# A two-layer hybrid encoder trunk: four places for the split weights, a fixed order of the first pieces, and conditioning sums on VectorE

## Chip, cores and metric

The kernel runs on one core of a Trainium2 chip. The metric is the device time of one execution in microseconds, lower is better. The profiled execution is one of several; every duration quoted below is of that one.

## What is computed

The reference is a trunk of two layers on 256 tokens of width 1024. Cut to what matters here:

```python
c_act = jax.nn.silu(c)                                   # c: 1 x 1024
for l in range(2):
    mod = c_act @ ada_w[l] + ada_b[l]                    # 1024 x 6144: the conditioning
    shift_m, scale_m, gate_m, shift_f, scale_f, gate_f = split(mod, 6)
    h = rms_norm(x, mix_norm_g[l]) * (1 + scale_m) + shift_m
    z = h @ w_in[l]                                      # 1024 x 7680: q, k, v of three mixers, and gates
    # differential, neighbourhood and dilated attention on parts of z
    merged = sum(sigmoid(gate_i) * (out_i @ w_proj_i))
    x = x + gate_m * (merged @ w_out[l])
    h = rms_norm(x, ffn_norm_g[l]) * (1 + scale_f) + shift_f
    x = x + gate_f * hier_moe(h)                         # 32 SwiGLU experts, top 2 within the best of 4 groups
return rms_norm(x, final_norm_g)
```

All weights are float32 in HBM, some 540 MB in all, and each is read once.

## The kernel before, in words

Each layer is a mixer stage and an expert stage. **The mixer** multiplies h by w_in in 15 chunks of 512 columns (function `chunk`); chunks 0 to 8 make q, k and v, chunks 9 to 14 the gates. A chunk's 2 MB of weights come as 1024x512 and are used in four pieces of 128x1024 elements. To keep float32 accuracy at TensorE's faster format, `split` (L322) makes two tiles of every piece: ScalarE casts it to `whi` (L327), VectorE subtracts to `wlo` (L330), and TensorE makes three products per block (`gemm`, L333): hi with whi, hi with wlo, lo with whi. A piece is 24 matmuls of 256 columns. `whi` and `wlo` have two buffers each (tags w4a, w4b), so a third piece can be split only when TensorE is done with the first. The two parts of h, `hi` and `lo`, are made by `modulated` (L277) for the eight 128-row blocks k: VectorE scales (L292), ScalarE adds the shift and rounds to hi (L294), VectorE makes lo (L289). Two pieces of chunk 0 are split ahead with GpSimd in place of VectorE for wlo (`early`).

`place` evacuates q and k with rotary embedding: four ScalarE copies per tile (L484), two VectorE multiplies (L485, L486) and a GpSimd addition (L487).

**The conditioning** is cut into 6 sections per layer, each of four parts of 1 MB (`ada_part`, L155). Sections 0 and 1 of layer 0 run at the start, on TensorE (L95, tile adap, with the silu of c as stationary operand of 32 columns). All others are mixed into the chunks by the table FILL: `ada_part` scales a part by c with ScalarE (L173) and VectorE (L175, 14 instructions of 128x512 per section), summing the parts of the section elementwise, and then sums over the 128 partitions with eight TensorE matmuls (adap<-rg,one), copies (L190), transposes (L193) and adds the bias (L195); the two gate sections go out to a row in HBM and come back as a broadcast tile `grb` (`gate_row`).

**The experts** (`moe`) read 8 groups of 12 tiles of 2 MB per layer (w13, w2g, w2c) and have little to compute on each.

Two things set the order. All DMAs of weights are issued by one queue (SP) in program order, each when a buffer is free: `slots` is a pool of 10 buffers of 16 KB per partition ("pairs"), which weights, conditioning parts and the long-lived tiles (xT, G, Q, K, V, T: six pairs in the mixer before) share; tiles of that pool all bear the name rg. And a list scheduler puts each engine's instructions in an order when the program is built; `keep_in_program_order` pins some of them. On the chip each engine runs its list in that order.

Of the kernel before, what the change touches and what calls it, by code (L numbers as in the profile page):

```python
# [21 lines left out]
P = 128  # L22
# [38 lines left out]
class Kernel:  # L61
# [91 lines left out]
    SEC = {0: ("col", 0), 1: ("col", 1), 2: ("row", 0), 3: ("col", 2), 4: ("col", 3), 5: ("row", 1)}  # L153

    def ada_part(self, l, s, h):  # L155

        nc = self.nc
        w = self.slot("ada").rearrange("p (j n) -> p j n", j=2)
        nc.sync.dma_start(w, self.io["ada_w"][l, s, h].rearrange("p (j n) -> p j n", j=2))
        kind, i = self.SEC[s]  # L160
        if h == 0:
            self.ada_ps = self.adap()
        ps = self.ada_ps[:, :256]
        if (l, s) in ((0, 0), (0, 1)):
            parts = [(w[:, j], self.scb[:, 2 * h + j, :], 2 * h + j) for j in range(2)]
        else:
            V = nc.vector
            for c in range(0, D, 512):
                cs = slice(c, c + 512)
                for j in range(2):  # L170
                    k, to = 2 * h + j, w[:, j, cs]
                    if j == 0 and h % self.CHAIN == 0:
                        nc.scalar.mul(to, to, self.sc[:, k:k + 1])  # L173
                    else:
                        V.scalar_tensor_tensor(to, to, self.sc[:, k:k + 1], w[:, 0, cs] if j else self.ada_sum[:, cs],  # L175
                                               op0=OP.mult, op1=OP.add)
            self.ada_sum = w[:, 1]
            parts = [(w[:, 1], self.one32, 2 * h + 1)] if (h + 1) % self.CHAIN == 0 else []
        for r, v, k in parts:
            ri = r.rearrange("p (m i) -> p i m", i=KD)  # L180
            for q in range(4):
                self.mm(ps[32 * q:32 * q + 32], v, ri[:, 2 * q:2 * q + 2, :] if s in (3, 4) else
                        r[:, 256 * q:256 * (q + 1)], k == 0 or k == 2 * self.CHAIN - 1 and v is self.one32, k == KD - 1)
        if h < 3:
            return
        if kind == "row":
            self.ada_row(l, i, ps, w[:, 0, :256])
            return
        sb = w[:, 0, :256]
# [188 lines left out]
    def mixer(self, l, fill):  # L378
# [63 lines left out]
        def chunk(n):  # L442
# [3 lines left out]
            if n == 4:  # L446
                late_loads()
# [681 lines left out]
```

## Time and profile before

| | before |
|---|---|
| time, median of 3 runs | 1534.49 us (1534.33 to 1534.7) |
| the profiled execution | 1535.39 us, of which the span shown is 1533.6 |
| TensorE (PE) busy | 1228.9 us, 80% |
| VectorE (DVE) busy | 606.8 us, 40% |
| ScalarE (ACT) busy | 384.7 us, 25% |
| GpSimd (POOL) busy | 73.4 us, 5% |
| HBM traffic | 543.93 MB, mean 355 GB/s |

The shares are means over stages that are unlike each other: two mixer stages (to about 345 us, and from 778 to 1095 us) and two expert stages. So the profile is read by stage. [...]

### The profile page before, as it was taken

Reading aid. Unit: us, or ns where it says so; the run is one execution under the profiler, and the core shown is the slowest. Engines: PE = TensorE matmul, PEld = TensorE weight load, DVE = VectorE, ACT = ScalarE, POOL = GpSimd, SP = SyncE. Lnnn points to the kernel's source line nnn. Section 1 sums busy time; section 2 is a strip of 40 time slices with the busy share of each in tenths; the row PEclk is TensorE's granted clock in tenths of the full one; section 3 lists DMA queues with packets and bytes.
Section 4 is the critical chain, followed back from the end, with each engine's and each line's share of the span. In section 5 each row is a group of like instructions: output and inputs, shape, how many; then the busy total and the mean of one; then the engine's idle time right before and its main releaser. Section 6 shows DMA issues by size and latency. Waiting matters only on the chain. (4 is left out here: it accounts for less than half of the span.)

```text
span 1533.6 us, 20114 instructions
## 1 busy us (share of the span) xinstructions
PE 1228.9 (80%) x8370; PEld 796.2 (52%) x8370; DVE 606.8 (40%) x1202; ACT 384.7 (25%) x681; POOL 73.4 (5%) x71
## 2 busy tenths in 40 slices
PE   5998999989777577677778899999897577577575
PEld 3888889874233133133257889899543133133132
DVE  2779884772112012011058797448322012011012
ACT  2656555450000000000046566544200000000001
POOL 1202000100000000000011110001000000000001
PEclk8999999999979889787889999999998788798898
DMA  9778683869999999999994874276899999999997
GB/s 369 284 296 319 275 326 146 343 246 403 428 425 427 427 427 427 427 426 428 421 372 172 340 312 186 110 315 235 318 425 426 427 426 427 427 426 427 426 427 294
DMA packets 52975, 543.93 MB, mean 355 GB/s; under 512 B 6784, under 2 KB 8336, under 8 KB 12048
## 3 DMA queue, kind: packets, MB, share of 16 engines
q1 hardware_dynamic: 52880, 542.60, 85.8%
q8 instruction: 68, 1.11, 0.3%
q14 instruction: 27, 0.22, 0.0%
HBM read 541.51 MB, written 1.06 MB: 354 GB/s over the span
## 5 line engine op out<-in xcount | busy, mean ns | idle before, releaser
L95 PE MATMUL acc<-rg,xg 128*32 128x512 f32 x2048 | 279.0, 687 | 116.3 <-DMA rg<-w 114.3
L95 PE MATMUL acc<-hi,wlo 128*128 128x256 f32 x896 | 260.0, 295 | 18.4 <-DVE wlo L330 18.0
L95 PE MATMUL acc<-lo,whi 128*128 128x256 f32 x896 | 253.4, 289 | 0.2 <-DVE lo L289 0.2
L95 PE MATMUL acc<-hi,whi 128*128 128x256 f32 x896 | 245.6, 290 | 6.5 <-ACT hi L294 4.9
L95 PE MATMUL acc<-rg,b 128*32 128x512 f32 (+1 forms) x1152 | 159.7, 688 | 93.7 <-DMA rg<-w2g 76.6
L95 PEld LDWEIGHTS acc<-rg,xg 128*32 128x32 f32 x2048 | 68.2, 118 | 303.7 <-issue 294.7
L330 DVE TENSOR_TENSOR wlo<-rg,whi 128x1024 fp32r<-128x1024 f32 x148 | 183.9, 1243 | 86.7 <-ACT whi L327 86.4
L327 ACT CAST whi<-rg 128x1024 fp32r<-128x1024 f32 x152 | 159.1, 1047 | 162.3 <-PE acc L95 136.1
L95 PEld LDWEIGHTS acc<-hi,wlo 128*128 128x128 f32 x896 | 175.1, 196 | 31.6 <-DVE wlo L330 24.2
L95 PEld LDWEIGHTS acc<-lo,whi 128*128 128x128 f32 x896 | 174.4, 196 | 1.6 <-DVE lo L289 0.5
L95 PEld LDWEIGHTS acc<-hi,whi 128*128 128x128 f32 x896 | 169.5, 196 | 10.5 <-ACT hi L294 5.5
L833 DVE TENSOR_TENSOR b<-b,acc 128x512 f32<-128x512 f32 x16 | 11.0, 687 | 350.5 <-PE acc L95 350.5
L95 PEld LDWEIGHTS acc<-rg,b 128*32 128x32 f32 x1152 | 35.5, 124 | 200.1 <-DMA rg<-w2g 112.6
L95 PEld LDWEIGHTS misc<-b,xn 128*128 128x128 f32 x512 | 124.6, 334 | 17.1 <-issue 15.7
L95 PE MATMUL misc<-b,xn 128*128 128x128 f32 x512 | 125.6, 404 | 4.1 <-DVEq L938 2.2
L832 ACT ACTIVATE b<-acc 128x512 f32<-128x512 f32 x16 | 9.6, 597 | 441.5 <-PE acc L95 441.5
L175 DVE SCALAR_TENSOR_TENSOR rg<-rg,sc 128x512 f32<-128x512 f32 x140 | 112.0, 832 | 4.4 <-DMA rg<-ada_w 2.5
L846 DVE TENSOR_TENSOR Y<-acc,grb 128x512 f32<-128x512 f32 x28 | 19.4, 692 | 235.5 <-PE acc L95 235.5
L826 ACT COPY b<-misc 128x256 f32<-128x256 f32 x16 | 6.0, 373 | 334.9 <-PE misc L825 334.9
L813 DVE TENSOR_SCALAR xg<-misc,mcol 128x128 f32<-128x128 f32 x128 | 44.3, 406 | 106.5 <-PE misc L95 106.5
L95 PE MATMUL acc<-wlo,hi 128*128 128x256 f32 (+1 forms) x256 | 79.8, 317 | 4.4 <-DVE wlo L330 4.3
L95 PE MATMUL acc<-whi,lo 128*128 128x256 f32 (+1 forms) x256 | 78.6, 314 | 1.5 <-DVE lo L310 1.3
(169 smaller groups left out, 1165.7 us busy)
## 6 DMA issues: line engine op xcount, KB each, us to landing
rg<-w SPq DMA_DIRECT2D x128, 2048.0 KB, 39.2
rg<-w2g SPq DMA_DIRECT2D x56, 2048.0 KB, 38.3
rg<-w_in SPq DMA_DIRECT2D x56, 1024.0 KB, 7.0
rg<-ada_w SPq DMA_DIRECT2D x48, 1024.0 KB, 8.5
rg<-w2c SPq DMA_DIRECT2D x12, 1024.0 KB, 29.6
rg<-w_proj SPq DMA_DIRECT2D x8, 1024.0 KB, 4.8
rg<-w_out SPq DMA_DIRECT2D x8, 1024.0 KB, 6.9
rg<-w_in SPq DMA_DIRECT2D x8, 512.0 KB, 15.4
```

The costliest lines, as they stand in the source:

```text
L95: return self.nc.tensor.matmul(out, lhsT, rhs, start=start, stop=stop, **kw)
L175: V.scalar_tensor_tensor(to, to, self.sc[:, k:k + 1], w[:, 0, cs] if j else self.ada_sum[:, cs], op0=OP.mult, op1=OP.add)
L327: c = nc.scalar.copy(whi, w)
L330: (nc.gpsimd if early else nc.vector).tensor_sub(wlo, w, whi.bitcast(F32))
L813: nc.vector.tensor_scalar(xg[:, k, :], p[:, kk * P:(kk + 1) * P], gf[:, k:k + 1], sf[:, k:k + 1], op0=OP.mult, op1=OP.add)
L826: nc.scalar.copy(ST, p[:, :256])
L832: nc.scalar.activation(a, h1, AF.Silu)
L833: nc.vector.tensor_mul(a, a, h3)
L846: nc.vector.tensor_mul(Y[:, hs], y[half], self.grb[:, hs])
```

## The change

- **Four places.** `split` takes its place from a list `homes`: during chunks 0 to 8 that is two halves of a pair ("parts") and the two old buffers in turn; later the old two alone. G shrinks to one long-lived tile (G2); the other two gate tiles are taken from the pool after the attention, in program order ("gates").
- **Order of the first pieces.** All four pieces of chunk 0 are split inside `modulated`, one before every second k, pinned in program order; wlo is always made by VectorE, none by GpSimd. One copy of xT goes from VectorE to ScalarE.
- **Conditioning.** ada_w lies transposed in HBM, so that one output is one row: c is broadcast to all partitions (`conditioning`, 512 KB, at the start and again in layer 1, as grb is overwritten by the gate rows in between), and VectorE multiplies and sums along the free axis with one `tensor_tensor_reduce` of 128x1024 for each half part (L166 of the new kernel; order lists show it as two rows, the operation and the read of its accumulator). No TensorE work, no transposes, no ScalarE scaling remains. Sections 0 and 1 of layer 0 are summed like the rest.

```diff
     def ada_part(self, l, s, h):
-        w = self.slot("ada").rearrange("p (j n) -> p j n", j=2)
...
-        if (l, s) in ((0, 0), (0, 1)):
-            parts = [(w[:, j], self.scb[:, 2 * h + j, :], 2 * h + j) for j in range(2)]
-        else:
-            V = nc.vector
-            for c in range(0, D, 512):
-                cs = slice(c, c + 512)
-                for j in range(2):
-                    k, to = 2 * h + j, w[:, j, cs]
-                    if j == 0 and h % self.CHAIN == 0:
-                        nc.scalar.mul(to, to, self.sc[:, k:k + 1])
-                    else:
-                        V.scalar_tensor_tensor(to, to, self.sc[:, k:k + 1], w[:, 0, cs] if j else self.ada_sum[:, cs],
-                                               op0=OP.mult, op1=OP.add)
...
+        w = self.slot("ada").rearrange("p (m k) -> p m k", m=2)
+        self.nc.sync.dma_start(w, self.io["ada_w"][l, s, h].rearrange("p (m k) -> p m k", m=2))
         if h == 0:
+            self.sums = self.cst.tile([P, KD], F32, name="sums", bufs=2)
+        for m in range(2):
+            self.ada_sum(w[:, m, :], self.sums[:, 2 * h + m:2 * h + m + 1])
+        if h == 3:
+            self.ada_done(l, s)
+    def ada_sum(self, w, to):
+        self.nc.vector.tensor_tensor_reduce(w, w, self.grb, scale=1.0, scalar=0.0, op0=OP.mult, op1=OP.add,
+                                            accum_out=to)
...
+    def conditioning(self):
+        self.nc.sync.dma_start(self.grb, bass.AP(tensor=self.io["c"].tensor, offset=0, ap=[[0, P], [1, D]]))
+        self.nc.scalar.activation(self.grb, self.grb, AF.Silu)
...
-            self.rest = lambda: self.tc.keep_in_program_order(nc.vector.tensor_copy(to, p))
+            self.rest = lambda: self.tc.keep_in_program_order(nc.scalar.copy(to, p))
...
         for k in range(KD):
+            if k % 2 == 0:
+                parts.append(self.split(w[k // 2], self.tc.keep_in_program_order))
             i = nc.vector.scalar_tensor_tensor(xT[:, k, :], xT[:, k, :], scale[:, k:k + 1], R,
                                                op0=OP.mult, op1=OP.mult)
             nc.scalar.activation(hi[:, k, :], xT[:, k, :], AF.Identity, bias=shift[:, k:k + 1])
-            if k > 1:
-                self.tc.keep_in_program_order(i)
+            self.tc.keep_in_program_order(i)
...
-    def split(self, w, early=False):
+    def split(self, w, keep=lambda i: None):
-        whi, wlo = (self.wk.tile([P, n, 1024 // n], F32R, name=f"{nm}{n}", tag=tag, bufs=2)
-                    for nm, tag in (("whi", "w4a"), ("wlo", "w4b")))
-        c = nc.scalar.copy(whi, w)
-        if early:
-            self.tc.keep_in_program_order(c)
-        (nc.gpsimd if early else nc.vector).tensor_sub(wlo, w, whi.bitcast(F32))
+        to = self.homes.pop(0)
+        self.homes.append(to)
+        if to is None:
+            whi, wlo = (self.wk.tile([P, n, 1024 // n], F32R, name=f"{nm}{n}", tag=tag, bufs=2)
+                        for nm, tag in (("whi", "w4a"), ("wlo", "w4b")))
+        else:
+            whi, wlo = (to[:, i:i + 1024].rearrange("p (k n) -> p k n", k=n).bitcast(F32R) for i in (0, 1024))
+        keep(nc.scalar.copy(whi, w))
+        keep(nc.vector.tensor_sub(wlo, w, whi.bitcast(F32)))
...
-        tiles = [self.slot("long") for _ in range(11)]
-        G, (Q0, Q1, K0, K1, V0, V1, T0, T1) = tiles[:3], tiles[3:]
+        G2, Q0, Q1, K0, K1, V0, V1, T0, T1 = take(9, "long")
+        self.homes = [self.slot("parts"), self.slot("parts"), None, None]
...
+            if n == 1 and l:
+                self.conditioning()
...
         self.dil_attention(l, qT, kT, vd, oT[1])
+        self.homes = [None]
+        G = take(2, "gates") + [G2]
+        ga += [G[i // 4][:, 512 * (i % 4):512 * (i % 4 + 1)] for i in range(12)]
         for n in range(9, 15):
             chunk(n)
```

The new kernel's lines are numbered anew: its split is L302 (ScalarE) and L303 (VectorE), scaling L263, lo L257, the rotary multiplies L462 and L463, the conditioning sums L166 and the bias L175.

**Place 1, VectorE at the start of layer 0**, from the end of the conditioning to the first blocks of h. Before:

```order
L190 COPY rg_162<-adap_144 128x256
L195 TENSOR_TENSOR mcol0_73<-adap_182,acol0_77 128x8
L214 SCALAR_TENSOR_TENSOR mcol0_73<-mcol0_73,gcol0_75 128x8
L292 SCALAR_TENSOR_TENSOR rg_187<-rg_187,mcol0_73,acc_262 128x256 x2
L289 SCALAR_TENSOR_TENSOR lo_247<-rg_187,mcol0_73,hi_246 128x256
L292 SCALAR_TENSOR_TENSOR rg_187<-rg_187,mcol0_73,acc_262 128x256
```

And now (rg_116 is the last pair of conditioning parts, rg_126 chunk 0's weights, rg_144 the pair "parts", rg_125 xT):

```order
L166 ISA rg_116,sums_110<-rg_116,grb_69 128x1024
L166 ISA sums_110 128x1
L175 TENSOR_TENSOR mcol0_74<-mcol0_74,sums_110 128x8
L303 TENSOR_TENSOR rg_144<-rg_126,rg_144 128x1024
L181 SCALAR_TENSOR_TENSOR mcol0_74<-mcol0_74,gcol0_76 128x8
L263 SCALAR_TENSOR_TENSOR rg_125<-rg_125,mcol0_74,acc_190 128x256 x2
L257 SCALAR_TENSOR_TENSOR lo_175<-rg_125,mcol0_74,hi_174 128x256 x2
L303 TENSOR_TENSOR rg_144<-rg_126,rg_144 128x1024
```

A subtraction of chunk 0 (L303) now stands ahead of the last conditioning step and of the first scaling, and another after every second block; the copy L190 is gone.

**Place 2, VectorE from the end of chunk 0 into chunk 1, layer 0** (before: rg_188 and rg_396 are the weights of chunks 0 and 1, rg_399 a conditioning part). Before:

```order
L330 TENSOR_TENSOR wlo2_369<-rg_188,whi2_368 128x1024
L330 TENSOR_TENSOR wlo2_409<-rg_396,whi2_408 128x1024
L485 TENSOR_TENSOR rg_194<-acc_290,rg_193 128x512
L486 TENSOR_TENSOR rg_197<-rg_197,rg_193 128x512
L330 TENSOR_TENSOR wlo2_437<-rg_396,whi2_436 128x1024
L485 TENSOR_TENSOR rg_194<-acc_291,rg_193 128x512
L486 TENSOR_TENSOR rg_197<-rg_197,rg_193 128x512
L330 TENSOR_TENSOR wlo2_465<-rg_396,whi2_464 128x1024
L175 SCALAR_TENSOR_TENSOR rg_399<-rg_399,sc_86 128x512 x3
L330 TENSOR_TENSOR wlo2_507<-rg_396,whi2_506 128x1024
```

And now (rg_328 and rg_460 are the weights of chunks 1 and 2, rg_331 conditioning parts):

```order
L303 TENSOR_TENSOR rg_144<-rg_328,rg_144 128x1024 x2
L257 SCALAR_TENSOR_TENSOR lo_175<-rg_125,mcol0_74,hi_174 128x256 x2
L303 TENSOR_TENSOR wlo2_391<-rg_328,whi2_390 128x1024
L166 ISA rg_331,sums_333<-rg_331,grb_69 128x1024
L166 ISA sums_333 128x1
L166 ISA rg_331,sums_333<-rg_331,grb_69 128x1024
L166 ISA sums_333 128x1
L303 TENSOR_TENSOR rg_144<-rg_460,rg_144 128x1024
L462 TENSOR_TENSOR rg_131<-acc_230,rg_125 128x512
L463 TENSOR_TENSOR rg_134<-rg_134,rg_125 128x512
L462 TENSOR_TENSOR rg_131<-acc_231,rg_125 128x512
L463 TENSOR_TENSOR rg_134<-rg_134,rg_125 128x512
```

Two pieces of chunk 1 are split before the last two lo blocks of chunk 0, and the first piece of chunk 2 before the fourth of chunk 1, which comes after a third conditioning sum below the last row; the rotary work of chunk 0 stands behind them.

**Place 3, VectorE and GpSimd at the start of layer 1.** Before, on VectorE:

```order
L239 SCALAR_TENSOR_TENSOR rsq_5075<-rsq_5075 128x2
L240 TENSOR_TENSOR rsq_5075<-rsq_5075 128x2
L241 TENSOR_TENSOR rsq_5075<-rsq_5075 128x2
L242 SCALAR_TENSOR_TENSOR rsq_5075<-rsq_5075 128x2
L272 COPY rg_4904<-acc_5037 128x512
L292 SCALAR_TENSOR_TENSOR rg_4904<-rg_4904,mcol1_74,acc_5087 128x256 x2
```

Before, on GpSimd in the same place (rg_5042 is chunk 0's weights):

```order
L247 MEMSET ssq4_9518 128x2
L330 TENSOR_TENSOR wlo2_5064<-rg_5042,whi2_5063 128x1024
L330 TENSOR_TENSOR wlo2_5068<-rg_5042,whi2_5067 128x1024
L487 TENSOR_TENSOR rg_5048<-rg_5048,rg_5051 128x512 x2
```

And now, on VectorE (rg_4855 is chunk 0's weights, rg_4873 the pair "parts"):

```order
L206 SCALAR_TENSOR_TENSOR rsq_4878<-rsq_4878 128x2
L207 TENSOR_TENSOR rsq_4878<-rsq_4878 128x2
L208 TENSOR_TENSOR rsq_4878<-rsq_4878 128x2
L209 SCALAR_TENSOR_TENSOR rsq_4878<-rsq_4878 128x2
L303 TENSOR_TENSOR rg_4873<-rg_4855,rg_4873 128x1024
L263 SCALAR_TENSOR_TENSOR rg_4717<-rg_4717,mcol1_75,acc_4890 128x256 x2
```

The two GpSimd subtractions are gone, the copy L272 has left VectorE, and one subtraction stands between the reciprocal root and the first scaling.

## Rows read from the trace of the kernel before

**Rows 1.** Windows by stage: length, busy us (x instructions) per engine, PEclk, DMA share, GB/s
```profile
49.00:164.00 115.00, 105.65 (x740) 94.22 (x739) 98.06 (x139) 69.05 (x108) 21.57 (x10) 0.97 0.73 286
164.00:345.00 181.00, 170.75 (x1326) 153.82 (x1325) 130.03 (x293) 94.29 (x174) 7.14 (x5) 0.98 0.69 266
345.00:778.00 433.00, 320.70 (x1975) 133.78 (x1967) 65.90 (x145) 16.97 (x40) 0.76 (x11) 0.87 1.00 424
...
801.00:931.00 130.00, 118.80 (x849) 105.67 (x849) 109.47 (x168) 77.36 (x124) 21.02 (x10) 0.99 0.68 269
931.00:1095.00 164.00, 155.15 (x1203) 141.54 (x1205) 100.78 (x228) 83.78 (x153) 7.01 (x4) 0.97 0.56 216
1095.00:1533.60 438.60, 310.90 (x1950) 129.62 (x1938) 67.86 (x156) 16.94 (x40) 5.73 (x8) 0.88 0.98 415
```

**Rows 2.** Chain that ended last, near its end: start us, length us, what
```profile
1437.26 39.16 DMA rg<-w
```

**Rows 3.** Timeline of the DMA queue around the first expert weights (rg<-w)
```profile
275.09 40.92 SPq L738 DMA_DIRECT2D rg<-w  x8
```

**Rows 4.** Timeline at the start of layer 0: start us, length us, engine, line, tiles, shape
```profile
25.94 1.61 PE L95 MATMUL adap<-rg,grb 128*32 128x256 f32 x16 [0.72 <-DMA rg<-ada_w]
...
28.72 1.07 PE L95 MATMUL adap<-rg,grb 128*32 128x256 f32 x16 [1.17 <-DMA rg<-ada_w]
...
31.09 4.66 POOL L330 TENSOR_TENSOR wlo<-rg,whi 128x1024 fp32r<-128x1024 f32 x2 [19.66 <-ACT whi L327]
31.15 2.31 DVE L214 SCALAR_TENSOR_TENSOR mcol<-mcol,gcol 128x8 f32<-128x8 f32 x1
...
34.66 0.58 PE L95 MATMUL acc<-hi,whi 128*128 128x256 f32 x1 [3.75 <-ACT hi L294]
```

**Rows 5.** Instruction groups by form, whole span, VectorE: busy us, mean ns, idle before
```profile
L330 DVE TENSOR_TENSOR wlo<-rg,whi 128x1024 fp32r<-128x1024 f32 x148 | 183.9, 1243 | 86.7 <-ACT whi L327 86.4
L175 DVE SCALAR_TENSOR_TENSOR rg<-rg,sc 128x512 f32<-128x512 f32 x140 | 112.0, 832 | 4.4 <-DMA rg<-ada_w 2.5 <-ACT rg L173 1.9
...
L679 DVE CUSTOM_DVE_ANT_0 rg<-misc,rg 128x512 f32<-128x512 f32 x16 | 11.0, 690 | 10.8 <-PE misc L95 10.8
...
L679 DVE DVE_READ_ACCUMULATOR2_ANT dl_s<- 128x1 f32 x16 | 1.3, 83 | 0.0
```

**Rows 6.** Timeline of VectorE in chunk 7: three conditioning steps back to back
```profile
127.89 2.07 DVE L175 SCALAR_TENSOR_TENSOR rg<-rg,sc 128x512 f32<-128x512 f32 x3
```

**Rows 7.** Timeline at the start of layer 1
```profile
779.59 4.64 POOL L330 TENSOR_TENSOR wlo<-rg,whi 128x1024 fp32r<-128x1024 f32 x2 [0.66 <-ACT whi L327]
```
**Rows 8.** The same stretch, VectorE
```profile
779.60 2.35 DVE L239 SCALAR_TENSOR_TENSOR rsq<-rsq 128x2 f32<-128x2 f32 x1
781.98 2.26 DVE L240 TENSOR_TENSOR rsq<-rsq 128x2 f32<-128x2 f32 x1
```
**Rows 9.** The same stretch, TensorE
```profile
787.09 0.58 PE L95 MATMUL acc<-hi,whi 128*128 128x256 f32 x1 [1.11 <-ACT hi L294]
```

**Rows 10.** TensorE groups by form, 49 to 164 us (chunks 1 to 8, layer 0)
```profile
L95 PE MATMUL acc<-hi,wlo 128*128 128x256 f32 x162 | 47.1, 295 | 8.7 <-DVE wlo L330 8.5
...
L95 PE MATMUL adap<-rg,one 128*32 128x256 f32 x24 | 3.5, 552 | 0.0
```

**Rows 11.** TensorE groups by form, 801 to 931 us (chunks 1 to 8, layer 1)
```profile
L95 PE MATMUL acc<-hi,wlo 128*128 128x256 f32 x189 | 55.1, 296 | 7.6 <-DVE wlo L330 7.5
...
L95 PE MATMUL acc<-wlo,hi 128*128 128x512 f32 x32 | 13.0, 405 | 3.6 <-DVE wlo L330 3.6
...
L95 PE MATMUL adap<-rg,one 128*32 128x256 f32 x32 | 4.1, 512 | 0.0
```

**Rows 12.** TensorE groups by form, 164 to 345 us (later chunks and attention, layer 0)
```profile
L95 PE MATMUL adap<-rg,one 128*32 128x256 f32 x24 | 3.1, 391 | 0.0
```

**Rows 13.** Finer windows inside chunks 1 to 8: columns as in Rows 1
```profile
109.00:151.00 42.00, 36.90 (x272) 33.52 (x271) 40.84 (x52) 23.93 (x34) 10.54 (x5) 0.92 0.73 289
...
871.00:881.00 10.00, 6.63 (x44) 6.43 (x43) 10.00 (x12) 5.56 (x9) 3.76 (x2) 0.83 0.71 290
```

More of the change, by code (lines that the diff above doesn't have):

```diff
@@ L179, in ada_part @@
[L179 to L189, printed above, removed]
@@ L211, in ada_done @@
-    def ada_done(self, l, s, i):
-        nc, m = self.nc, self.mcol[l][:, i, :]
+    def ada_done(self, l, s):
+        nc, i = self.nc, self.SEC[s]
+        m = self.mcol[l][:, i, :]
+        nc.vector.tensor_add(m, m, self.sums)
+        if s in (2, 5):
+            if s == 2:
+                nc.vector.tensor_scalar(m, m, 0.5, None, op0=OP.mult)
+            nc.sync.dma_start(self.grow[2 * l + i - 4].rearrange("(p m) -> p m", p=P), m)
         if s in (1, 4):
@@ L299, in modulated @@
         low(KD - 1)
-        return hi, lo
+        return hi, lo, parts
     def to_hilo(self, src, done):
@@ L395, in mixer, with take @@
         M = self.xT.rearrange("p k n -> p (k n)")
-        tiles = [self.slot("long") for _ in range(11)]
-        for b in tiles:
-            nc.gpsimd.memset(b[:, 2047:2048], 0.0)
-        G, (Q0, Q1, K0, K1, V0, V1, T0, T1) = tiles[:3], tiles[3:]
-        ga = [G[i // 4][:, 512 * (i % 4):512 * (i % 4 + 1)] for i in range(12)]
+        def take(n, of):
+            tiles = [self.slot(of) for _ in range(n)]
+            for b in tiles:
+                nc.gpsimd.memset(b[:, 2047:2048], 0.0)
+            return tiles
+        G2, Q0, Q1, K0, K1, V0, V1, T0, T1 = take(9, "long")
+        self.homes = [self.slot("parts"), self.slot("parts"), None, None]
+        ga = []
         tok = [M[:, t * D:(t + 1) * D] for t in range(2)]
@@ L425, in mixer @@
                     hs = slice(half * 512, (half + 1) * 512)
-                    self.square(t, half, self.x[:, t, hs], G[t][:, hs])
+                    self.square(t, half, self.x[:, t, hs], (T0, T1)[t][:, hs])
             for c in range(4):
                 self.raw_t(c)
-        halves = [self.split(w0[0][:, k:k + 2], True) for k in (0, 2)]
-        hi, lo = self.modulated(l)
+        hi, lo, halves = self.modulated(l, [w0[k // 4][:, k % 4:k % 4 + 2] for k in range(0, KD, 2)])
         def late_loads():
@@ L445, in chunk @@
                 nc.sync.dma_start(self.rope, io["rope"])
+            if n == 1 and l:
+                self.conditioning()
             if n == 4:
@@ L471, in chunk @@
             if n == 0:
-                pieces[:2] = [(*p, h) for p, h in zip(pieces, halves)]
+                pieces = [(*p, h) for p, h in zip(pieces, halves)]
             self.gemm(pieces, hi, lo, prods)
```

60 lines of the change are left out of this document (15 added, 45 removed).

## The prediction, made before the changed kernel was run

> **What bounds the kernel now.** I read the windows by stage first. In the two expert stages the DMA engines are full (share 1.00 and 0.98, 424 and 415 GB/s), and in the mixers they are not (0.56 to 0.73) while TensorE is 91 to 95% busy [rows 1]. The chain that ended last is made of expert weights to nearly the end [rows 2]. So an expert stage lasts as long as its bytes do, and its start is set by the mixer: its first eight tiles are issued over 41 us near the mixer's end [rows 3], one by one as the mixer gives buffers back. A microsecond taken out of a mixer therefore moves the expert stage behind it, and the end, by about a microsecond. This holds while the mixer's DMA share stays well under 1, which the windows show.
>
> Inside the mixers two engines come into question. In chunks 1 to 8 of layer 0 (49 to 164 us) TensorE is busy 105.65 of 115 us and VectorE 98.06; in layer 1 (801 to 931) 118.80 and 109.47 of 130 [rows 1]. TensorE's idle time there is mostly the wait for wlo: 8.7 us in layer 0 [rows 10], 7.6 + 3.6 = 11.2 us in layer 1 [rows 11]. The finer windows tell why: from 109 to 151 us VectorE is busy 40.84 of 42 us, and TensorE 36.90, with the granted clock at 0.92; from 871 to 881 VectorE is busy the whole 10 us and TensorE 6.63, clock 0.83 [rows 13]. There VectorE is the bound, not the number of buffers. Over the whole stretches VectorE still has 17 and 20.5 us to spare, so part of the wait is a matter of who may work ahead.
>
> **The change part by part.** The sum is made against the profiled execution, 1535.4 us, 0.9 above the median of the runs, 1534.5.
>
> *A conditioning step on VectorE.* A section costs 14 instructions of L175 before. Three back to back take 2.07 us, 0.69 each, so 9.7 us; by the mean of 832 ns, which holds waits for GpSimd, it is 11.6 [rows 5, 6]. After it is 8 sums of 1024 columns. No row shows a reduce with both inputs in SBUF. The nearest are the reduce L679, 690 ns for 512 columns plus 83 ns for the accumulator, with one input in PSUM, and L330, a plain two-input operation of 1024 columns, 1243 ns [rows 5]. Two halves of the first give 1.38 us, L330 and an accumulator read 1.33: I take 1.33, so 10.6 us per section. The difference to before, -1.0 to +0.9 us per section, I set at 0.
>
> [...] In L175 both tensor inputs are float32 in SBUF, and three of them take 0.69 us each for 512 columns, as the reduce with PSUM does [rows 5, 6]. [...]
>
> *Start of layer 0.* The broadcast of c is 512 KB more, in the queue ahead of all parts. Parts of 1 MB come 2.78 us apart at the end [rows 4], so +1.4 us on the last landing. Behind it before: from 28.72 to 34.66 us, of which L214, an operation of 128x8, took 2.31 us because GpSimd's split held VectorE up (POOL 31.09 to 35.75) [rows 4]. After: two sums (2.7 us; each pair fits the 2.78 us between parts, so no backlog) in place of matmuls, copy, transposes and add (about 2.4), then no GpSimd (-2.15), but one wlo of 1.24 in front of the scaling (place 1). Sum 1.4 + 0.3 - 2.15 + 1.24 = +0.8. In chunk 0 VectorE then makes four wlo instead of two, +2.5 us, among sixteen scalings and lo's; against that, the pieces of chunk 1 are split earlier. I take +1 (from -1 to +3).
>
> *Start of layer 1.* Two tiny operations take 2.35 and 2.26 us beside the 4.64 us of GpSimd's split [rows 7, 8]; an accumulator read, one column wide, takes 83 ns [rows 5], so left alone the two should need no more than 0.3. So 4.3 us come off the way to the first matmul at 787.09 [rows 9], the copy L272 leaves it (512 columns, 0.69 by L175 of the same width), one wlo (1.24) enters (place 3): -3.75. The second broadcast of c lies ahead of chunk 1's weights but is hidden by the matmuls of chunk 0. VectorE's two additional wlo are partly in chunk 0 again. I take -4 (from -6 to 0).
>
> *Four places in chunks 1 to 8.* What can be won is bounded below by nothing, and above by the waits for wlo and the conditioning's matmuls: layer 0 8.7 + 3.5 = 12.2 us [rows 10], layer 1 11.2 + 4.1 = 15.3 [rows 11]. VectorE must still do its 98 and 109 us, and GpSimd's ten rotary additions still stand beside it. Four places let it be two more pieces ahead, 2 x 1.24 = 2.5 us of its work, each time it has been idle before a dense stretch. In layer 0 there is one dense stretch of 42 us with 5.1 us of TensorE idle and some 3 us of clock loss (0.08 of 42 us) [rows 13]: 2.5 to 4 of it go, and about 3 of the smaller waits: -6. In layer 1 the dense stretches are short, like that at 871, where 3.4 us of TensorE are lost within 10 [rows 13], so a lead of 2.5 us covers most of each: -8. The new order (place 2) puts three sums and four rotary operations ahead of chunk 1's fourth subtraction, so a wait of 1 to 3 us there stays. That TensorE takes the first piece of the next chunk in such a gap is what the four places allow.
>
> *Conditioning's TensorE work in the second half.* 3.1 us between 164 and 345 us [rows 12], in a stretch where TensorE is busy 170.75 of 181 us and VectorE 130 [rows 1]: here it is TensorE that bounds, so -3 (from 0 to -5 with the transposes, which aren't in the row). In layer 1 all four sections lie in chunks 1 to 8 and are counted above. ScalarE's scaling (L173) is gone, but ScalarE is busy about half of the time: 0.
>
> *G as late tiles.* A pair is taken from the pool between the end of "parts" and the gates, and may for a chunk or two leave three pairs for weights. The mixer's DMA share of 0.69 hides it: 0 (to +3).
>
> Sum: +1 - 4 - 6 - 8 - 3 = -20, so 1515.4 by the profiled execution and **1514** by the median.
>
> **The rivals.**
>
> 1. *VectorE eats the lead.* If the dense stretches decide everything, four places win nothing in chunks 1 to 8, and only the starts and the second half remain: +1 - 4 - 3 = -6, and a microsecond or two of small waits: 1528. For it: 40.84 of 42 us. Against it: 17 and 20 us of idle VectorE in the same chunks.
>
> 2. *All waits go*: +1 - 6 - 12.2 - 15.3 - 5 and some 5 us of clock: 1492. It would need VectorE at 95% in its fixed order; only one stretch does that.
>
> [...]
>
> [...]
>
> 4. *The change does not do what it says*: the built order pins VectorE and ScalarE so that chunk 1's fourth piece, and its like in each chunk, come as late as before, and the sums stand in front of the subtractions. Then the gain at layer 1's start is used up by the heavier chunk 0: 1532 to 1538.
>
> **How the numbers follow.** Forecast (1500 to 1524) 0.55; rival 1 (1524 to 1532) 0.17; rival 2 0.07; rival 3 0.11, anywhere above 1538; rival 4 0.10. About 0.2%, 3 us, is what a measurement of this kernel can tell from no change. Faster is the forecast, rivals 1 and 2: 0.79, less the little of rival 1 above 1531.4, plus as much of rival 4. Same is most of rival 4, 0.08. Slower is rival 3 and the rest of 4: 0.13. The range 1496 to 1537 holds the forecast, rival 1, rival 4 and the slow part of 2: about 0.82.
>
> **What would show it.** In the profile after: the sums at 1.3 us (rival 3 if 2 or more); the first matmul of layer 0 at 35 to 36 us, and of layer 1 within 5 us of the reduce of the sums of squares; no VectorE operation of two columns above 0.3 us at either start; waits of TensorE for wlo in chunks 1 to 8 down to some 4 us per layer; the expert stages as long as before. I would be wrong if VectorE stood above 95% in all chunks 1 to 8, if a wait for w_in or ada_w appeared in VectorE's or ScalarE's rows, or if an expert stage changed its length.

## The result: 1507 us, and errors that partly cancelled

The changed kernel takes 1507.24 us (median of 4 runs, 1506.97 to 1507.89); the kernel before, on the same chip, 1534.6. The ratio is 0.9822, interval 0.9805 to 0.9839: 27 us less, where 20 were forecast, and inside the range. Several of the terms behind it were not right, as the marks below and twelve more kernels show.

Windows of the changed kernel, columns as in [rows 1], PEclk being the clock granted to TensorE as a share of full speed; the profiled execution has a span of 1506.0 us:

```profile
49.00:149.00 100.00, 96.92 (x703) 91.39 (x702) 91.02 (x127) 59.42 (x87) 18.12 (x12) 0.98 0.78 314
...
240.00:285.00 45.00, 38.48 (x231) 31.62 (x230) 16.08 (x35) 16.99 (x33) 0.00 (x0) 0.70 0.44 174
779.00:891.00 112.00, 108.22 (x797) 102.90 (x798) 101.59 (x141) 70.71 (x101) 18.16 (x12) 0.99 0.79 314
```

The first and the last line are chunks 1 to 8 (in layer 1 with chunk 0): TensorE is idle 3.1 and 3.8 us there, against 9.35 and 11.2 in [rows 1]. Two windows of the kernel before that answer to the last two lines:

```profile
240.00:285.00 45.00, 43.43 (x349) 38.77 (x348) 21.88 (x44) 24.45 (x45) 0.00 (x0) 1.00 0.54 210
787.00:917.00 130.00, 118.72 (x838) 107.43 (x839) 108.06 (x150) 77.48 (x119) 21.02 (x10) 0.97 0.70 279
```

TensorE's groups that wait for wlo, layer 0 (two lines), then layer 1:

```profile
L95 PE MATMUL acc<-hi,wlo 128*128 128x256 f32 x86 | 24.8, 291 | 2.5 <-DVE wlo L303 2.5
L95 PE MATMUL acc<-wlo,hi 128*128 128x512 f32 x16 | 6.4, 397 | 0.3 <-DVE wlo L303 0.3
...
L95 PE MATMUL acc<-hi,wlo 128*128 128x256 f32 x96 | 27.1, 285 | 2.4 <-DVE wlo L303 2.4
L95 PE MATMUL acc<-wlo,hi 128*128 128x512 f32 x16 | 6.6, 410 | 1.3 <-DVE wlo L303 1.3
```

2.8 and 3.7 us, where [rows 10] and [rows 11] had 8.7 and 11.2. Half of the pieces now lie in the pair "parts", which bears the name rg; TensorE's groups that read it show no wait for VectorE in these two windows, so the sums are of all pieces. VectorE's groups by form, changed kernel:

```profile
L303 DVE TENSOR_TENSOR wlo<-rg,whi 128x1024 fp32r<-128x1024 f32 x116 | 145.0, 1250 | 59.1 <-ACT whi L302 58.1 <-DMA rwg<-rw 0.5 <-DMA rg<-w 0.4
L166 DVE CUSTOM_DVE_ANT_0 rg<-rg,grb 128x1024 f32<-128x1024 f32 x96 | 118.6, 1274 | 10.0 <-DMA rg<-ada_w 9.8
L303 DVE TENSOR_TENSOR rg<-rg 128x1024 fp32r<-128x1024 f32 x36 | 47.8, 1338 | 2.4 <-ACT rg L302 2.2 <-DMA rg<-dmask 0.2
L166 DVE DVE_READ_ACCUMULATOR2_ANT sums<- 128x1 f32 x96 | 7.7, 80 | 0.0
```

A sum takes 1.27 us and the read of its accumulator 0.08 (1.33 forecast for both). The starts, VectorE and TensorE, first layer 0, then layer 1:

```profile
30.14 1.22 DVE L166 CUSTOM_DVE_ANT_0 rg<-rg,grb 128x1024 f32<-128x1024 f32 x1
...
31.41 0.17 DVE L175 TENSOR_TENSOR mcol<-mcol,sums 128x8 f32<-128x8 f32 x1
31.49 1.22 DVE L303 TENSOR_TENSOR rg<-rg 128x1024 fp32r<-128x1024 f32 x1
32.63 0.16 DVE L181 SCALAR_TENSOR_TENSOR mcol<-mcol,gcol 128x8 f32<-128x8 f32 x1
...
34.04 1.22 PE L95 MATMUL acc<-hi,rg 128*128 128x256 f32 x4 [10.49 <-ACT hi L265]
...
774.74 0.16 DVE L223 TENSOR_REDUCE rstd<-ssq 128x2 f32<-128x10 f32 x1 [0.64 <-ACT misc L218]
...
778.90 1.22 PE L95 MATMUL acc<-hi,rg 128*128 128x256 f32 x4 [1.59 <-ACT hi L265]
```

The operation of 128x8 that [rows 4] show at 2.31 us now takes 0.16. From the reduce to layer 1's first matmul it is 4.2 us; before it was 8.5, from this row to 787.09 [rows 9]:

```profile
778.61 0.16 DVE L256 TENSOR_REDUCE rstd<-ssq 128x2 f32<-128x10 f32 x1 [0.64 <-ACT misc L251]
```

### Where the 27.6 us of the spans lie

I use five marks of the trace: a layer's first matmul of chunk 0; ScalarE's first copy of chunk 8's values; its last Tanh (the last gate); its last copy from the dilated attention; its last split in the mixer. Differences from before to after, from the rows at full digits:

| stretch | before, us | after, us | difference |
|---|---|---|---|
| to layer 0's first matmul | 34.7 | 34.0 | -0.6 |
| from there to chunk 8's copy | 131.1 | 114.9 | -16.2 |
| from there to the last attention copy | 114.3 | 128.3 | +13.9 |
| from there to the last split | 45.6 | 45.6 | -0.1 |
| to layer 1's reduce | 452.9 | 452.0 | -0.9 |
| reduce to first matmul, layer 1 | 8.5 | 4.2 | -4.3 |
| from there to chunk 8's copy | 130.1 | 111.6 | -18.5 |
| from there to the last split | 155.5 | 156.4 | +0.9 |
| to the end | 460.9 | 459.1 | -1.8 |

Layer 1 keeps what its chunks win; layer 0 gives 14 of 16 us back before the dilated attention ends. ScalarE at that place, before:

```profile
271.66 0.59 ACT L467 ACTIVATE rg<-acc 128x512 f32<-128x512 f32 x1
...
280.11 0.27 ACT L691 COPY rg<-misc 128x128 f32<-128x128 f32 x1 [0.43 <-PE misc L95]
```

and after, with rows of TensorE:

```profile
245.78 1.89 PE L95 MATMUL misc<-rg 128*64 128x128 f32 x16
...
248.72 0.59 ACT L444 ACTIVATE rg<-acc 128x512 f32<-128x512 f32 x1
...
252.30 1.09 PE L560 MATMUL misc<-k,rg 128*128 128x128 f32 x4 [3.64 <-DVE rg L663]
253.32 6.59 PE L95 MATMUL misc<-rg 128*64 128x128 f32 x28
...
262.36 1.08 PE L560 MATMUL misc<-k,rg 128*128 128x128 f32 x4 [1.41 <-DVE rg L663]
...
277.17 0.27 ACT L671 COPY rg<-misc 128x128 f32<-128x128 f32 x1 [1.31 <-PE misc L95]
```

The last gate (L444) comes 23 us earlier than before, the last attention copy only 3. Between the two TensorE has nothing but the attention's small matmuls and some transposes: the attention is uncovered, where "covered" means that it runs among the gates' matmuls. It waits for the softmax (3.64 us ahead of 252.30, 1.41 ahead of 262.36), and its clock falls to 0.70 from 240 to 285 us, though it counts as busy for 38.48 of 45 us: the same small matmuls take 118 ns each at 245.78, where the granted clock is 1.00 (245.8 to 247.7 us), and 235 ns each at 253.32, where it is 0.50 (253.3 to 259.9 us), twice as long.

### The profile page after: what moved, and what is told of

The parts are those of the page before. It is cut to its first block, busy times and chain, and to the rows that moved or that the text cites. A ratio compares the mean times of both kernels' runs of the same rounds, so it can differ in the third digit from the quotient of the medians.

```text
span 1506.0 us, 19652 instructions
## 1 busy us (share of the span) xinstructions
PE 1198.5 (80%) x8146; PEld 787.0 (52%) x8146; DVE 614.6 (41%) x1246; ACT 372.2 (25%) x664; POOL 57.5 (4%) x67
## 5 line engine op out<-in xcount | busy, mean ns | idle before, releaser
L95 PE MATMUL acc<-hi,wlo 128*128 128x256 f32 x704 | 200.2, 289 | 7.9 <-DVE wlo L303 7.7
L95 PE MATMUL acc<-lo,whi 128*128 128x256 f32 x704 | 196.1, 284 | 0.0
L95 PE MATMUL acc<-hi,whi 128*128 128x256 f32 x704 | 191.4, 286 | 1.2 <-ACT whi L302 1.1
L303 DVE TENSOR_TENSOR wlo<-rg,whi 128x1024 fp32r<-128x1024 f32 x116 | 145.0, 1250 | 59.1 <-ACT whi L302 58.1
L302 ACT CAST whi<-rg 128x1024 fp32r<-128x1024 f32 x116 | 121.5, 1047 | 107.4 <-PE acc L95 99.2
L95 PEld LDWEIGHTS acc<-hi,wlo 128*128 128x128 f32 x704 | 135.1, 192 | 15.3 <-DVE wlo L303 11.6
L95 PEld LDWEIGHTS acc<-rg,b 128*32 128x32 f32 x1152 | 33.9, 120 | 197.1 <-DMA rg<-w2g 105.1
L95 PEld LDWEIGHTS acc<-lo,whi 128*128 128x128 f32 x704 | 134.5, 192 | 1.4 <-issue 1.0
L95 PEld LDWEIGHTS misc<-b,xn 128*128 128x128 f32 x512 | 124.6, 334 | 16.9 <-issue 15.5
L95 PEld LDWEIGHTS acc<-hi,whi 128*128 128x128 f32 x704 | 131.0, 192 | 2.9 <-ACT whi L302 2.1
L166 DVE CUSTOM_DVE_ANT_0 rg<-rg,grb 128x1024 f32<-128x1024 f32 x96 | 118.6, 1274 | 10.0 <-DMA rg<-ada_w 9.8
L95 PE MATMUL acc<-hi,rg 128*128 128x256 f32 x384 | 74.6, 293 | 13.1 <-ACT hi L265 12.1
L95 PEld LDWEIGHTS acc<-hi,rg 128*128 128x128 f32 x384 | 62.7, 201 | 14.4 <-ACT hi L265 12.6
```

What stands on the lines that cost most here:

```text
L95: return self.nc.tensor.matmul(out, lhsT, rhs, start=start, stop=stop, **kw)
L166: self.nc.vector.tensor_tensor_reduce(w, w, self.grb, scale=1.0, scalar=0.0, op0=OP.mult, op1=OP.add, accum_out=to)
L302: keep(nc.scalar.copy(whi, w))
L303: keep(nc.vector.tensor_sub(wlo, w, whi.bitcast(F32)))
```

## The experiments

The profile's marks for all kernels, in order of the text, in us, differences from full digits (C8: from first matmul to chunk 8's copy; gate, att, split: last Tanh, last attention copy and last split of layer 0; L1: from the last split of layer 0 to that of layer 1):

| kernel | median, us | ratio to before, 95% | C8 layer 1 | gate | att | split | L1 |
|---|---|---|---|---|---|---|---|
| before | 1533 to 1535 | | 130.1 | 271.7 | 280.1 | 325.8 | 746.9 |
| changed | 1507.2 | 0.9822 [0.9805, 0.9839] | 111.6 | 248.7 | 277.2 | 322.7 | 724.1 |
| e1 | 1541.2 | 1.0044 [1.0027, 1.0060] | 143.6 | 276.2 | 279.4 | 324.9 | 754.0 |
| e2 | 1556.3 | 1.0137 [1.0119, 1.0154] | 146.1 | 289.4 | 286.9 | 336.1 | 761.3 |
| e5 | 1509.3 | 0.9841 [0.9816, 0.9866] | 116.1 | 252.9 | 268.2 | 313.7 | 732.3 |
| e6 | 1516.2 | 0.9889 [0.9868, 0.9911] | 112.1 | 258.0 | 272.2 | 317.9 | 733.6 |
| e3 | 1510.2 | 0.9845 [0.9828, 0.9861] | 112.2 | 275.5 | 278.7 | 324.3 | 724.4 |
| e4 | 1498.1 | 0.9766 [0.9750, 0.9782] | 112.2 | 259.4 | 263.5 | 309.0 | 723.6 |
| e8 | 1510.7 | 0.9848 [0.9828, 0.9869] | 112.2 | 255.2 | 279.6 | 325.2 | 725.8 |
| e11 | 1504.4 | 0.9809 [0.9793, 0.9826] | 114.3 | 264.6 | 267.8 | 313.3 | 728.9 |
| e7 | 1534.4 | 1.0010 [1.0000, 1.0020] | 143.4 | 269.9 | 273.0 | 318.6 | 751.7 |
| e10 | 1565.1 | 1.0206 [1.0189, 1.0223] | 146.8 | 297.3 | 289.0 | 344.0 | 757.7 |
| e12 | 1537.2 | 1.0009 [0.9994, 1.0023] | 130.7 | 255.0 | 286.6 | 332.6 | 744.1 |
| e9 | 1507.8 | 0.9832 [0.9815, 0.9848] | 112.3 | 248.8 | 276.8 | 322.4 | 724.1 |

Wherever the attention copy comes last in layer 0 (all but e2 and e10), the last split follows 45.5 to 46.0 us behind it. In those kernels the end of that mixer is set by the end of its dilated attention; in e2 and e10 the last gate ends later, and the last split follows it by 46.7 us.

### What each part is worth: e1, e2, e5, e6

e1, two places:

```diff
-        self.homes = [self.slot("parts"), self.slot("parts"), None, None]
+        take(2, "parts")
+        self.homes = [None]
```

> The changed kernel with two places for the weights' parts all through (the two additional tiles are still taken from the pool, and stand empty). The prediction's terms: the places bring 6 us in layer 0 and 8 in layer 1, so about 1521 us. The trace of the changed kernel: chunks 1 to 8 ended some 16 us earlier in each layer, but layer 0 gave it back at the end of its mixer; if all of that is the places' work, two places cost nothing in layer 0 and 15 to 19 us in layer 1: 1522 to 1526. If the conditioning's new form is what made the chunks shorter and the places bring little: under 1512.

e2, the same and the old start (GpSimd for two pieces, the rest split in chunk 0):

```diff
-        hi, lo, halves = self.modulated(l, [w0[k // 4][:, k % 4:k % 4 + 2] for k in range(0, KD, 2)])
+        halves = [self.split(w0[0][:, k:k + 2], self.tc.keep_in_program_order, nc.gpsimd) for k in (0, 2)]
+        hi, lo = self.modulated(l)
```

> As the kernel with two places, and the start of each layer as before: two pieces' parts from GpSimd, the other two of chunk 0 split in the chunk, the copy of the last transposed block on VectorE. Against the kernel before, only the conditioning's new form (and the later taking of G) is left of the change. The prediction's terms: starts together 3 us, so 3 us slower than two places alone, and the conditioning alone 3 to 6 us faster than before: about 1524 to 1530. By the marks in the trace (first matmul of layer 0 0.6 us earlier, of layer 1 4.9 earlier relative to the mixer's start): 5.5 us slower than two places alone.

e5 and e6 begin from the kernel before. e5 takes over the four places, the late G and the new start, and keeps L175's steps and their sums on TensorE; e6 takes over the places and the late G alone:

```diff
+        self.homes = [self.slot("parts"), self.slot("parts"), None, None]
...
+        self.homes = [None]
+        G = take(2, "gates") + [G2]
```

> The kernel before with four places, G's two tiles taken late and the new start of each layer, but with the conditioning as before (steps of 512 columns on VectorE, sums across partitions on TensorE). Against the changed kernel it lacks the new conditioning alone. The prediction held the new conditioning for a gain of about 3 us (and up to 11 with all its TensorE work in both layers): then 1510 to 1518. With two places it cost 22 us (the kernel with two places and the old start stands at 1556, before at 1534). If that cost is its own and stays with four places: 1483 to 1490. If four places absorb it, because a pair of sums of 2.6 us in VectorE's queue then no longer holds up the piece that TensorE waits for: 1503 to 1512.

> The kernel before with four places and G's two tiles taken late, and nothing else: old conditioning, old start. The prediction's terms: 14 us for the places, so 1520 to 1521. By the runs with two places, where the places took 34 us off: 1500 to 1510. The distance to the kernel with the old conditioning and the new start is what the start is worth: 3 us by the prediction, 15 by the runs with two places.

e1 and e2 lie above all that was expected of them, e5 in its third range, e6 between its two. From before to the changed kernel there are thus two ways, each step a difference of two medians:

| | conditioning first | places first |
|---|---|---|
| new conditioning | +22.6 (e2) | -2 (changed, from e5) |
| new start | -15.2 (e1, from e2) | -6.9 (e5, from e6) |
| four places | -33.9 (changed, from e1) | -16.9 (e6) |

The forecast had -3, -3 and -14. On the right-hand way it comes near, within the intervals, and -2 can't be told from nothing. But that -2 is a sum of two larger parts. Against e5, the changed kernel's last split of layer 0 comes 9.0 us later (322.7 and 313.7; its attention ends 28 us behind the last gate, e5's 15), layer 1 from split to split is 8.2 us shorter, and the rest 2.7. On the left-hand way each of its three terms is wrong: with two places the new conditioning makes the kernel slower than before, by more than the forecast of the whole gain. The parts don't add. Between the profiled spans of e2 and e1 there are 18.4 us (15 between the medians). Of these, 3.9 and 4.4 lie ahead of the layers' first matmuls (37.8 against 33.9; 460.4 against 456.0 us from layer 0's last split), and the rest in the chunks, where the order differs too; I have not split it further.

e6 also shows what the places do by themselves, at the start and with the conditioning of before. Its window from layer 1's first matmul to chunk 8's copy:

```profile
778.20:890.26 112.06, 110.19 (x803) 102.11 (x804) 100.96 (x130) 71.40 (x103) 21.32 (x12) 0.98 0.72 287
```

TensorE is idle for 1.9 us there, against 11.3 in the window of before from 787 to 917 us, and the stretch is 18.0 us shorter; 5.7 of these come back between chunk 8's copy and the last split.

### Layer 0's lost gain: e3, e4, e8, e11

e3, four places in layer 1 alone: `self.homes = p + [None, None] if l else [None]`, with p the two tiles.

> The changed kernel with four places in layer 1 and two in layer 0. Theory: in layer 0 the time that the places win in chunks 1 to 8 is lost again in the dilated attention, which the built order puts behind the last gate chunk; with two places the order has it among the gate chunks again. So 1504 to 1511, about as the changed kernel (1507). Rival: the places' gain in layer 0 arrives at the end, and without it the loss in the attention would be larger still: 1515 to 1523.

1510.2: four places in layer 0, which win 16 us up to chunk 8, are worth 3 at the end, and the intervals of the two kernels overlap. With two places there the last gate and the attention end together (275.5 and 278.7).

e4 and e8 change only how many parts of the conditioning each chunk of layer 0 takes, and the built order with it:

```diff
-    FILL = (0, 1, 0, 3, 0, 2, 2, 3, 2, 2, 3, 2, 3, 0, 1), ...
+    FILL = (0, 1, 0, 3, 0, 2, 2, 3, 2, 1, 0, 0, 0, 2, 3), ...    (e4)
+    FILL = (0, 1, 0, 3, 0, 2, 2, 3, 0, 0, 0, 0, 2, 3, 3), ...    (e8)
```

> The changed kernel, four places in both layers; only the numbers of conditioning parts per chunk of layer 0 differ (chunks 9 to 14 take 1, 0, 0, 0, 2, 3 in place of 2, 3, 2, 3, 0, 1; the rest comes behind chunk 14). The built order then has all but the last of the dilated attention among the gate chunks 13 and 14. Theory (the uncovered attention and its low clock took 13 to 20 us at the end of mixer 0): 1490 to 1500, and the granted clock of the stretch before the last gate's end back to 0.95 or more. Rival (the mixer's end in layer 0 waits for something else, such as the transfers of the expert weights or VectorE's total work, which is the same): 1505 to 1510. A second rival: the parts that now come late hold up the buffers of the first expert weights: 1510 to 1520.

> The changed kernel with four places and no conditioning part at all in chunks 8 to 11 of layer 0 (chunks 8 to 14 take 0, 0, 0, 0, 2, 3, 3, the rest comes behind). VectorE is freer between 145 and 200 us than in any other kernel here, yet the built order has six of the eight softmaxes of the dilated attention behind the last gate chunk, against two to four in the kernel that took 1498 us. Theory that the order decides (an uncovered attention, at the low clock): 1503 to 1512. Rival that VectorE's load in chunks 8 to 12 held the attention up: 1490 to 1499.

Windows of e4, then e8 (two), then the changed kernel:

```profile
240.00:285.00 45.00, 43.42 (x360) 40.65 (x359) 27.99 (x42) 20.40 (x33) 7.04 (x4) 1.00 0.89 359
```
```profile
240.00:285.00 45.00, 40.10 (x259) 33.65 (x259) 17.57 (x37) 19.03 (x37) 0.00 (x0) 0.77 0.47 186
145.00:200.00 55.00, 50.84 (x380) 47.79 (x379) 38.90 (x97) 29.38 (x66) 0.00 (x0) 0.94 0.62 244
```
```profile
145.00:200.00 55.00, 52.13 (x398) 48.38 (x397) 52.47 (x118) 29.43 (x62) 1.96 (x1) 1.00 0.91 374
```

In e4 the clock stays at 1.00 in that window, attention and gates end together (263.5 and 259.4), the last split comes 13.7 us earlier than in the changed kernel, and the whole takes 1498.1 us: faster than both kernels. (The profiled execution is the fastest of e4's four, 1493.5, so 9 us by the medians is the figure to keep.) VectorE's load between 145 and 200 us is not the cause: in e8 it has 16 us of air there, where the changed kernel has 2.5, and yet the attention ends at 279.6, 24 us behind the last gate, at a clock of 0.77, and the time is 1510.7. Nor is its load between 200 and 240 us, where it is busy 23.6 of 40 us in the changed kernel, 35.3 in e4 and 35.9 in e8. What e4 has and e8 lacks is an order in which the softmaxes stand among the gates' matmuls. The first operation of the last of the dilated attention's eight softmaxes, and the last gate, in e4 and then in e8:

```profile
256.92 0.69 DVE L659 CUSTOM_DVE_ANT_0 rg<-misc,rg 128x512 f32<-128x512 f32 x1 [0.21 <-PE misc L95]
259.36 0.60 ACT L444 ACTIVATE rg<-acc 128x512 f32<-128x512 f32 x1
```
```profile
272.57 0.69 DVE L659 CUSTOM_DVE_ANT_0 rg<-misc,rg 128x512 f32<-128x512 f32 x1 [1.58 <-PE misc L95]
255.18 0.59 ACT L444 ACTIVATE rg<-acc 128x512 f32<-128x512 f32 x1
```

None of the eight begins behind the last gate in e4, four do in e8 and in the changed kernel, two in the kernel before.

e11 has another such order (FILL 0, 1, 1, 3, 1, 2, 2, 3, 2, 0, 0, 0, 0, 2, 3).

> The changed kernel with other numbers of conditioning parts per chunk of layer 0 (0, 1, 1, 3, 1, 2, 2, 3, 2, 0, 0, 0, 0, 2, 3, the rest behind). The built order has all eight softmaxes of the dilated attention ahead of the last gate's evacuation, one more than in the kernel that took 1498 us. If the uncovered attention is what separates 1507 from 1498: 1490 to 1498. If what is left in that kernel lies elsewhere: 1497 to 1503.

1504.4 misses both expectations. The attention is covered (3 us behind the last gate, clock 1.00), but chunk 8's copy comes at 153.7 us, in e4 at 147.9: with the additional parts in chunks 2 and 4 TensorE waits for a wlo twice for long:

```profile
86.32 0.39 PE L95 MATMUL acc<-hi,wlo 128*128 128x256 f32 x1 [3.12 <-DVE wlo L303]
...
137.92 0.38 PE L95 MATMUL acc<-hi,wlo 128*128 128x256 f32 x1 [3.27 <-DVE wlo L303]
```

From 34 to 150 us it waits 7.3 us for wlo in all, in e4 3.0. So a covered attention alone does not give e4's time. From split to split, layer 1 also takes 5 us longer than in e4, 3.1 of them ahead of its first matmul and 2.1 in its chunks up to 8; I can't explain that.

e7, two places with e4's numbers:

> Two places, with the numbers of conditioning parts of the kernel in which the dilated attention is covered. Theory: the uncovered attention is a consequence of chunks that end early; with two places the attention was covered already (1541), so the numbers change little: 1535 to 1543. Rival: fewer sums in chunks 9 to 12 are a gain of their own, because VectorE is nearly full from 145 to 200 us: 1525 to 1533.

1534.4, 7 us better than e1, just below the first expectation and above the second. So a part of what the numbers bring does not need the places; in layer 0 e7's last split comes 6.3 us ahead of e1's, e4's 13.7 ahead of the changed kernel's.

### Why the new sums cost so much with two places: e10, e12

In e1 between two subtractions of layer 1, VectorE and then TensorE (rows of the accumulators left out):

```profile
812.09 1.22 DVE L166 CUSTOM_DVE_ANT_0 rg<-rg,grb 128x1024 f32<-128x1024 f32 x1
...
817.82 1.22 DVE L166 CUSTOM_DVE_ANT_0 rg<-rg,grb 128x1024 f32<-128x1024 f32 x1
...
818.97 1.21 DVE L303 TENSOR_TENSOR wlo<-rg,whi 128x1024 fp32r<-128x1024 f32 x1
...
820.23 0.56 PE L95 MATMUL acc<-wlo,hi 128*128 128x512 f32 x1 [3.92 <-DVE wlo L303]
```

Six sums stand in one row, 6.9 us, and TensorE waits 3.92 for the wlo behind them. Over layer 1's chunks 0 to 8, sums stand between 13 of 35 successive subtractions, mostly in pairs that hold VectorE for 2.3 us. In the kernel before, L175's steps were spread: between 23 of 33, for 0.7 to 2.7 us (once for 5.1).

e10 cuts each sum in two of 512 columns: `for q in range(2): self.ada_sum(w[:, m, qs], self.grb[:, qs], ...)`.

> The kernel with two places (1541 us), with each sum cut in two of 512 columns (two accumulators, added at the section's end). Theory: the new conditioning is slow with two places because a sum holds VectorE for 1.3 us, a pair for 2.6, while TensorE waits for the next piece; steps of 0.69 us can be placed between: 1525 to 1534, though VectorE has more instructions. Rival: the length of a step does not matter, the order of the pieces and of the attention does: 1538 to 1548.

1565.1, slower than both expectations. It is no test of the theory, though: the halves stayed together (mostly four of them, 2.45 us, where a pair stood, and twelve in a row, 7.35 us, where six did), and they are dearer, 192 of them at 718 ns plus a read each.

e12 holds the order instead: the sums wait in a list (`owed`), and `pay` takes one of them behind each piece's subtraction, two while more than four are owed.

```diff
             whi, wlo = done[0] if done else self.split(w)
+            if not done:
+                self.pay(2 if len(self.owed) > 4 else 1)
...
-        self.nc.vector.tensor_tensor_reduce(w, w, self.grb, ...)
+        self.tc.keep_in_program_order(self.nc.vector.tensor_tensor_reduce(w, w, self.grb, ...))
```

> The kernel with two places (1541 us), with the sums held to one after each piece's subtraction (two where a chunk has more than two parts), in place of pairs and fours. In the traces so far VectorE has 1.5 to 2.5 us of conditioning between nearly any two subtractions before the change, and with the new sums 2.6 us between some, up to 9 behind a late weight, and none between others. Theory: with two places TensorE waits for each lump, so evenly spread sums bring back most of what the new conditioning cost in chunks 1 to 8 of layer 1: from layer 1's first matmul to the copy of chunk 8's values 130 to 136 us (143.7 with two places, 130.1 before), last split of layer 1 735 to 748 us behind that of layer 0 (754.1). The end of layer 0's mixer is no test, since the built order has the dilated attention behind the last gate there; the whole may be 1530 to 1545 us. Rival: the grouping doesn't matter, the new sums cost as much wherever they stand: 141 us or more to chunk 8's values, 752 or more from split to split.

Layer 1's windows from first matmul to chunk 8's copy and TensorE's waits for wlo, e1 first, then e12:

```profile
781.00:925.00 144.00, 122.48 (x816) 111.61 (x817) 111.05 (x172) 74.82 (x114) 20.78 (x12) 0.93 0.72 284
```
```profile
L95 PE MATMUL acc<-hi,wlo 128*128 128x256 f32 x192 | 57.4, 303 | 9.6 <-DVE wlo L303 9.5
L95 PE MATMUL acc<-wlo,hi 128*128 128x512 f32 x32 | 13.9, 434 | 6.8 <-DVE wlo L303 6.8
```
```profile
788.00:919.00 131.00, 118.58 (x810) 107.91 (x811) 107.35 (x158) 74.65 (x113) 20.77 (x12) 0.96 0.69 276
```
```profile
L95 PE MATMUL acc<-hi,wlo 128*128 128x256 f32 x192 | 57.0, 301 | 6.3 <-DVE wlo L314 6.1
L95 PE MATMUL acc<-wlo,hi 128*128 128x512 f32 x31 | 12.8, 412 | 1.3 <-DVE wlo L314 1.2
```

130.7 us in place of 143.6, 744.1 from split to split in place of 754.0: the theory's values in both. VectorE spends about as long on its sums in both stretches (39.7 us in e1, 40.4 in e12, where six of 32 come behind chunk 8's copy), so in layer 1 the grouping is what made them dear, not their total. In layer 0 the new order left the attention uncovered (255.0 to 286.6), as its expectation said, and that took the gain away again.

### The reduce's price: e9

`tensor_tensor_reduce(...)` becomes `scalar_tensor_tensor(w, w, 1.0, self.grb, op0=OP.mult, op1=OP.mult, accum_out=to)`; the order of every engine stays.

> The changed kernel with each sum written as a scalar-tensor-tensor with an accumulator (times 1, times c) in place of the tensor-tensor-reduce; every engine's order is as in the changed kernel. [...] Otherwise (this form costs what the reduce costs): 1.2 to 1.35 us each, 1504 to 1511 us.

VectorE's group in e9:

```profile
L166 DVE SCALAR_TENSOR_TENSOR rg<-rg,grb 128x1024 f32<-128x1024 f32 x96 | 118.6, 1273 | 10.2 <-DMA rg<-ada_w 10.1
```

1273 ns and 1507.8 us: the same. Neither form shows a mean of 2 us or more, the sign of rival 3: both take about as long as a plain subtraction of the same width (L303, 1250 ns).

## Why the prediction was right, and where it was not

- **The sums** (1.33 us with the read): 1.27 and 0.08. Right. No run shows a mean of 2 us or more, to which the prediction gave 0.11 as rival 3: it is 1274 ns for the reduce and 1273 for the scalar-tensor-tensor (e9).
- **Start of layer 0** (+1): -0.6. GpSimd's hold (2.31 us for the operation of 128x8, now 0.16) and the wlo in front (1.22) came as worked out. The +1.7 for the broadcast of c and the longer sums was too much: the scale was ready at 31.6 in place of 31.1, +0.5. So the first matmul came at 34.0 us, ahead of the 35 to 36 that were to show the forecast.
- **Start of layer 1** (-4): -4.3 to the first matmul. Right there, but not shown for what lies behind: with the conditioning of before, the old start (e6) and the new one (e5) take the same time from the reduce to chunk 8's copy, 120.5 and 120.3 us.
- **Four places, layer 1** (-8, at most -15.3): -18.5 for the stretch, with the conditioning that left TensorE; 0.9 came back behind it. The size was wrong, more than twice the -8. The waits for wlo went to 3.7 us, as "some 4" foresaw. The upper bound was too low because it summed waits and conditioning alone. Between the two marks of that stretch TensorE's busy time fell by 11.1 us: 3.7 are the conditioning's matmuls and transposes, 2.4 are 16 small matmuls that now stand outside the stretch, and the other 5 are the same products, each a little shorter (hi with whi 293 ns before and 284 with whi after, at a clock of 0.97 and 0.98). The reading "There VectorE is the bound, not the number of buffers" is not borne out over the stretch as a whole: e6 has VectorE do the same splits and steps of conditioning as before, changes the places, and takes 18.0 us less.
- **Four places, layer 0** (-6), **and TensorE's conditioning in the second half** (-3): -16.2 up to chunk 8, and 13.9 back behind it. The step that failed is "A microsecond taken out of a mixer therefore moves the expert stage behind it, and the end, by about a microsecond", used for a microsecond out of chunks 1 to 8 as if it were one out of the mixer. From 164 to 345 us I read TensorE's 170.75 of 181 us as the bound [rows 1]. But there were two chains in that stretch, the gates' matmuls and the attention, and in the trace of before the attention was already the later, by 8.4 us (280.1 against 271.7). Time won ahead of the gates reaches the end only if the attention moves too, as e4 and e8 show. I had named the order of VectorE and ScalarE as a rival, but not TensorE's.
- **The conditioning on VectorE** (0): beside four places the total comes out so, by luck: 9.0 us lost in layer 0 against 8.2 and 2.7 won later (e5). The reasoning (the same busy time, so the same cost) fails: with two places the same work, in larger groups, cost 22 us. For layer 1 e12 shows that it is the grouping; for layer 0 no run does. The places bring twice as much with the new conditioning (33.9) as without it (16.9).
- **G late** (0): nothing shows against it; e6, which has it, gained.
- **The other signs**: no operation of two columns takes over 0.3 us at either start, VectorE is busy 91% of chunks 1 to 8 in both layers, and the expert stages keep their length. Waits for weights, which I called a sign of being wrong, do appear in a small form: ScalarE waits 3.5 us for a w_in at 51 us and VectorE 2.5 us for an ada_w at 890 us.

So 12 us forecast for layer 1 were 23, 8 for layer 0 were 3, and the sum came out near. The mechanism of the places (they give VectorE a lead, and TensorE's waits go) is shown by e1 and e6; that the start with GpSimd off it is worth something, by e5 against e6 and e1 against e2. That the sum of the parts came out near was luck.

## What to carry to other kernels

Before a gain in one stage is carried to the end, look for the chain that runs beside the stage behind it, and compare where both end: the later one decides, and here what ended early left the other alone, at a lower clock (0.70 in the changed kernel, 1.00 in e4). Work that is moved onto an engine that runs its list in order was priced here by how it is grouped between the results that someone waits for (e1 and e12: 143.6 and 130.7 us to chunk 8's copy, with sums of 39.7 and 40.4 us), and by how many places those results have (e1 and the changed kernel: 143.6 and 111.6 us), not by its sum alone. A planner's table (here the parts per chunk) is to be tuned again once a change moves the stages against each other: e4 gave 9 us that way.

## What was not expected of the hardware

TensorE counts as busy for 38.48 of 45 us in a stretch of small, dependent matmuls, and the granted clock is 0.70 there, against 1.00 in e3 for the same attention among gate chunks:

```profile
240.00:285.00 45.00, 43.89 (x360) 40.23 (x359) 21.88 (x39) 23.43 (x41) 0.00 (x0) 1.00 0.50 197
```

Being uncovered costs twice here, in waits (3.64, 1.41 and 1.47 us for the softmax) and in matmuls of double length (118 and 235 ns). And a reduction along 1024 columns took VectorE about as long as an elementwise operation (1274 and 1250 ns): successive sums start 1.15 us apart with the read of the accumulator (0.08 us) in between.
